# A hybrid decoder block on one core: lora products at full height with zero-padded weights, parameters read behind x, and other starting times for the planner

## The chip, the cores and the metric

The kernel runs on one core of a Trainium2 chip. The metric is the device time of one execution in microseconds (us). The engines have one queue each: TensorE (PE in the profile; PEld are its weight loads) does matrix products, VectorE (DVE), ScalarE (ACT) and GpSimd (POOL) do elementwise work, and SyncE (SP) issues the transfers (DMA) between the core's memory and HBM.

## What is computed

The reference is one decoder layer over 512 positions of width 1024: two token mixers side by side, merged by gates, and behind them a gated feed-forward layer with a short convolution. The part that the change touches is the decay and the gate `a` of the RWKV mixer; `wz` and `az` have 64 columns each, the results have 1024:

```python
z_r = z_r + rwkv_mu * (_shift1(z_r) - z_r)
rr, kr, vr, wz, az, gz = _split(z_r, [RWKV_DIM, RWKV_DIM, RWKV_DIM, W_LORA, A_LORA, G_LORA])
w_log = -jax.nn.softplus(-(rwkv_w0 + jnp.tanh(wz) @ rwkv_w2).astype(F32)) - 0.5
decay = jnp.exp(-jnp.exp(w_log))
a = jax.nn.sigmoid((rwkv_a0 + az @ rwkv_a2).astype(F32))
...
y = _rwkv7_scan(r_h, w_h, k_r, v_r, -kk, kk * a_h)
...
h = h + _rmsnorm(mix, attn_post_norm[l])
```

All of it is float32. The kernel gets that precision from products in the chip's faster float32 form (`fp32r`) by splitting each operand into a high part and a remainder: three products in place of one for the large matrices, two for the lora matrices.

## The kernel before

**Stages.** A first stage (line L399 for all of its engine instructions, since a helper records them) loads x and the parameters, splits x into `xuh` and `xul`, computes the first five column blocks of the input product into `zps`, and the norm of x. Then comes the mixer stage (line L243): 8 blocks of 128 channels (`hb`, called heads here, though each holds two RWKV heads of 64), and for each the input products of K, R, V, F, Q, G and VN (24 products with 512 columns into `zps`, or products with 256 columns into `vps`), an RWKV front, a triangular solve, an RWKV chain over 8 chunks (products into `us` and `yp`), and the HGRN mixer (`hsc`, `ups`, `ops`). 16 gate blocks and three blocks of the branch product close the stage. Behind it come the branch products, the output product and the feed-forward layer, which are not planned anew.

**What sets the order.** In the first stage the order is that of the code. In the mixer stage a planner (class `Plan`) interleaves eight generators at build time: it keeps an assumed time at which each engine is free (`at`), an assumed cost for each operation and an assumed delay between engines, and emits whichever operation can start first by its own reckoning. What it emits is then fixed: on each engine the instructions run in that order, and each waits for its inputs. `AT0` holds the assumed times at which VectorE, ScalarE and GpSimd come free, counted from the moment at which TensorE does (zero).

**The lora products.** `zwah` holds the 64 rows of tanh(wz) above the 64 rows of az, high parts; `zws` and `zas` hold remainders in one half and a second copy of the high part in the other. For each head, `front(hb)` loads the two 64-row weight matrices twice, one copy under the other (`lwr`), ScalarE makes the high part (`lw`), and GpSimd overwrites one half of it with the remainder. A product of 64 rows (`lw[0:64]` by `zwah[0:64]`) and one of 128 rows (`lw` by `zws`) are summed in `wps`; the same for `aps` with the other half.

**The first loads.** SyncE issues the transfers of the first stage in one queue: two weight blocks in halves, 8 columns of parameters, x in 8 tiles (`xt`), and the other 290 columns of parameters (`pr`) ahead of x's tiles 3 to 7. On VectorE `consts()`, twelve small operations that read those 290 columns, stands ahead of the remainders `xul` of tiles 3 to 7.

Of the kernel before, what the change touches and what calls it, by code (L numbers as in the profile page):

```python
# [8 lines left out]
F32 = mybir.dt.float32  # L9
F32R = mybir.dt.float32r  # L10
# [6 lines left out]
P = 128  # L17
# [21 lines left out]
NPRM = _off  # L39
# [5 lines left out]
RAWS = 1  # L45
WAIT, PEN = 1.0, 0.07
MARGIN = 0.8
AT0 = (5.5, 2.5, 0.0)
XG = ((0, 0),)
MORD = ((0, 0), (1, 0), (2, 0), (3, 0), (0, 1), (1, 1), (2, 1), (3, 1))  # L50
WOT = (7.0, 9.2, 13.5, 15.0)
# [235 lines left out]
def block_kernel(ctx: ExitStack, tc: tile.TileContext, out: bass.AP, xT: bass.AP, xN: bass.AP,  # L287
# [3 lines left out]
    nc = tc.nc  # L291
# [8 lines left out]
    pr = const.tile([P, NPRM], F32, name="pr")  # L300
# [5 lines left out]
    def pcs(name):  # L306
        o, w = PCOLS[name]
        return pr[:, o : o + w]
# [74 lines left out]
    pers = ph1.enter_context(tc.tile_pool(name="pers", bufs=1))  # L383
# [17 lines left out]
    Vi, Gi, Ai, Ti = Chain(V, "Vi"), Chain(G, "Gi"), Chain(A, "Ai"), Chain(T, "T")  # L401
# [39 lines left out]
    Gi.memset(r17[:, :, :, 0:1], 1.0)  # L441
    scm = pers.tile([P, NT, P], F32, name="scm")
    lwr0 = pers.tile([P, 2 * P], F32, name="lwr0")
    Gi.memset(sgx[:, :, 0:1], 0.0)
    Gi.memset(scm, 0.0)

# [13 lines left out]
    def consts():  # L460
        Vi.tensor_scalar(cm, pr[:, o_mu : o_mu + 26], -1.0, 1.0, op0=ALU.mult, op1=ALU.add)
        Vi.tensor_single_scalar(hw0, pcs("w0"), 0.5, op=ALU.mult)
        Vi.tensor_single_scalar(ha0, pcs("a0"), 0.5, op=ALU.mult)
        Vi.tensor_single_scalar(hka, pcs("k_a"), 0.5, op=ALU.mult)
        Vi.tensor_scalar(oka, pcs("k_a"), -0.5, 1.0, op0=ALU.mult, op1=ALU.add)
        Vi.tensor_single_scalar(nkk, pcs("k_k"), -1.0, op=ALU.mult)
        Vi.tensor_single_scalar(hkk, pcs("k_k"), 0.5, op=ALU.mult)
        Vi.tensor_single_scalar(lnw8, pcs("ln_w"), 8.0, op=ALU.mult)
        Vi.tensor_single_scalar(gn5, pcs("gnorm"), 0.5, op=ALU.mult)
        Vi.tensor_tensor(lmx, pcs("lb0"), pcs("lb1"), op=ALU.max)  # L470
        Vi.tensor_tensor(le[:, 0], pcs("lb0"), lmx, op=ALU.subtract)
        Vi.tensor_tensor(le[:, 1], pcs("lb1"), lmx, op=ALU.subtract)
# [38 lines left out]
    with tc.tile_pool(name="init", bufs=1) as ip, tc.tile_pool(name="pinit", bufs=1, space=PSUM) as pi:  # L511
# [26 lines left out]
        def init_wh(b, dst, src=None):  # L538
            raw = wraw.tile([P, 1024], F32, name="raw", tag="raw")
            nc.sync.dma_start(raw, win[b] if src is None else src)  # L540
            hi, lo = dst
            w0.append(dst)
            wlast["hi"] = Ai.copy(hi, raw)
            wlast[V] = Vi.tensor_tensor(lo, raw, hi.bitcast(F32), op=ALU.subtract)
# [6 lines left out]
        def half_load(i, c):  # L551
            hc = slice(c * 512, c * 512 + 512)
            nc.sync.dma_start(raws0[i][:, hc], win[(B_WA, B_GZ)[i]][:, hc])

        def half_split(i, c, eng, key):
            hc = slice(c * 512, c * 512 + 512)
            hi, lo = w0[i]
            wlast["hi"] = Ai.copy(hi[:, hc], raws0[i][:, hc])
            wlast[eng] = key.tensor_tensor(lo[:, hc], raws0[i][:, hc], hi[:, hc].bitcast(F32), op=ALU.subtract)

        def init_x(k):
            Ai.activation(xuh[:, k], xt[:, k], AF.Identity, scale=pc("g_pre", k))
            Vi.scalar_tensor_tensor(xul[:, k], xt[:, k], pc("g_pre", k), xuh[:, k].bitcast(F32),
                                    op0=ALU.mult, op1=ALU.subtract)

        def init_s(k):
            x2 = acc[k] if k < 2 else ip.tile([P, S], F32, name="x2", tag="xr", bufs=6)
            Ai.activation(x2, xt[:, k], AF.Square)
            if k > 1:
                Vi.tensor_tensor(acc[k % 2], acc[k % 2], x2, op=ALU.add)  # L570
            if k == KD - 1:
                Vi.tensor_tensor(acc[0], acc[0], acc[1], op=ALU.add)
# [15 lines left out]
            nc.sync.dma_start(xt[:, k], xT[:, k])  # L588
        half_load(0, 1)
        half_load(1, 1)  # L590
        nc.sync.dma_start(pr[:, 8:NPRM], prm[:, 8:NPRM])
        for k in range(3, KD):
            nc.sync.dma_start(xt[:, k], xT[:, k])
        half_split(0, 0, V, Vi)
        init_x(0)
        half_split(1, 0, V, Vi)
# [1 line left out]
            init_x(k)  # L598
        half_split(0, 1, V, Vi)
        half_split(1, 1, V, Vi)  # L600
        consts()
        for k in range(3, KD):
            init_x(k)
            if k >= LAG:
                init_s(k - LAG)
        init_wh(B_K, wi[0])
        for k in range(KD - LAG, KD):
            init_s(k)
# [65 lines left out]
    V1, G1, A1, T1, D1 = Lazy(V, "V"), Lazy(G, "G"), Lazy(A, "A"), Lazy(T, "T"), Lazy(nc.sync, "D")  # L674
    for k_ in "VGA":
        last[k_] = last[k_ + "i"]
    plan = Plan(seq, RANKS, BONUS, (0.0,) + AT0 + (0.0,))

# [29 lines left out]
    zwah = pers.tile([P, S], F32R, name="zwah")  # L708
# [4 lines left out]
    hs = (slice(0, 64), slice(64, 128))  # L713
# [35 lines left out]
    def front(hb):  # L749
        lwr = lwr0  # L750
        if hb > 0:
            yield D1.dma_start(lwr, wlg[hb, :, 0 : 2 * P])
        lw = mx.tile([P, 2 * P], F32R, name="lw")
        yield A1.copy(lw, lwr)
        for h in range(2):
            q, c = hs[1 - h], slice(h * P, h * P + P)
            yield G1.tensor_tensor(lw[q, c], lwr[q, c], lw[q, c].bitcast(F32), op=ALU.subtract)
        yield done(("K", hb), "zwa")
        fin.add(("go", hb))
        k = kt[hb]  # L760
        wps = pf.tile([P, S], F32, name="wps", tag="f")
        yield T1.matmul(wps, lw[0:64, 0:P], zwah[0:64], start=True, stop=False)
        yield T1.matmul(wps, lw[:, 0:P], zws, start=False, stop=True)
        sg = sgx
        yield A1.activation(sg[:, :, 1:65], c8(wps), AF.Tanh, scale=0.5, bias=hw0[:, hb : hb + 1])
        yield V1.tensor_single_scalar(sg[:, :, 1:65], sg[:, :, 1:65], 1.0, op=ALU.add)
        aps = pf.tile([P, S], F32, name="aps", tag="f")
        yield T1.matmul(aps, lw[64:128, P : 2 * P], zwah[64:128], start=True, stop=False)
        yield T1.matmul(aps, lw[:, P : 2 * P], zas, start=False, stop=True)
        cum = mx.tile([P, NCH, 65], F32, name="cum")  # L770
        yield V1.tensor_tensor_scan(cum.rearrange("p n c -> p (n c)"), m65.rearrange("p n c -> p (n c)"),
# [501 lines left out]
    plan.spawn("evac", lora_in())  # L1273
    plan.spawn("evac", first_in())
    plan.spawn("front", chained(front, lambda hb: []))
    plan.spawn("chain", chained(chain, lambda hb: [("solve", hb), "zgz"]))
    plan.spawn("hgrn", chained(hgrn, lambda hb: [("F", hb)]))
# [339 lines left out]
```

## Time and profile before

| | before |
|---|---|
| median of 3 runs | 1190.23 us (1187.6 to 1190.32) |
| the profiled execution, its own time | 1188.11 us |
| its span, from the first to the last instruction | 1186.4 us |
| PE busy | 1154.1 us (97% of the span) |
| DVE, ACT, POOL busy | 60%, 44%, 46% |
| DMA, mean over the span | 100 GB/s |

Times below are counted from the span's start. Matmuls are pipelined, so the busy time of one is longer than its slot; the slot is the distance from one start to the next. "Idle" is the time in which an engine had nothing to run, with what ended it behind the arrow; that name is taken from the semaphore that changed last and is sometimes that of another instruction that ended at the same moment. PEclk is the granted share of TensorE's full clock of 2.4 GHz, so that 0.50 is its lower level, 1.2 GHz.

### The profile page before, as it was taken

To read this page: it belongs to the slowest core of one execution; us is meant where nothing else is said; L and a number is where in the kernel's file an instruction comes from. 1 tells how busy PE (TensorE), PEld (TensorE's weight loads), DVE (VectorE), ACT (ScalarE), POOL (GpSimd) and SP (SyncE) were. 2 spreads that over 40 slices of the span, in tenths; PEclk is the share of its full clock that TensorE was granted. 3 is DMA by queue.
4 is the path that set the end of the run, shared out by engine and by line. 5 is a ranking of instruction groups with operands and counts; after the bars stand their busy time and mean duration, and the time that the engine had idled before them with its cause. 6 is when DMAs were issued, how large, how long until landed. Compare 5 with 4: busy or idle time off the path is not lost. (4 is left out here: it accounts for less than half of the span.)

```text
span 1186.4 us, 19408 instructions
## 1 busy us (share of the span) xinstructions
PE 1154.1 (97%) x7336; PEld 951.2 (80%) x7336; DVE 717.4 (60%) x1599; ACT 522.4 (44%) x1010; POOL 540.5 (46%) x572
## 2 busy tenths in 40 slices
PE   9998999999999999999999999999999999999997
PEld 7776797877878787788888778888888888888786
DVE  6898888889878778987747535445422322232213
ACT  7634355454545454454544532245433343434221
POOL 2254345353344434334343655402856575657521
PEclk9999999999999999999999999999999999999999
DMA  5212222122222131323242584373322232323232
GB/s 187 72 54 68 80 63 79 50 66 89 70 72 61 54 108 43 98 70 94 67 136 64 186 276 161 112 243 125 107 89 89 89 107 82 123 81 111 88 104 89
DMA packets 57390, 118.85 MB, mean 100 GB/s; under 512 B 22097, under 2 KB 25297, under 8 KB 57297
## 3 DMA queue, kind: packets, MB, share of 16 engines
q1 hardware_dynamic: 57296, 117.62, 31.7%
q8 instruction: 58, 0.95, 0.3%
q14 instruction: 36, 0.29, 0.1%
HBM read 104.22 MB, written 13.37 MB: 99 GB/s over the span
## 5 line engine op out<-in xcount | busy, mean ns | idle before, releaser
L243 POOL TENSOR_TENSOR wlo_t<-raw,whi_t 128x256 fp32r<-128x256 f32 x280 | 226.2, 836 | 294.8 <-ACT whi_t L243 264.6
L324 POOL TENSOR_TENSOR wlo_t<-raw,whi_t 128x1024 fp32r<-128x1024 f32 x75 | 182.2, 2436 | 84.0 <-ACT whi_t L324 83.8
L243 PE MATMUL zps<-xl,whi_t 128*128 128x512 f32 x488 | 198.4, 406 | 0.0
L243 PE MATMUL zps<-xh,wlo_t 128*128 128x512 f32 x488 | 198.1, 406 | 0.0
L243 PE MATMUL zps<-xh,whi_t 128*128 128x512 f32 x488 | 198.0, 406 | 0.0
L324 ACT CAST whi_t<-raw 128x1024 fp32r<-128x1024 f32 x77 | 80.1, 1048 | 153.4 <-DMA raw<-wup 66.6
L1478 DVE SCALAR_TENSOR_TENSOR u<-zps,pr,u 128x511 f32<-128x511 f32 x40 | 30.0, 750 | 188.1 <-ACT u L1477 184.6
L366 PE MATMUL zps<-x2h,whi_t 128*128 128x512 f32 x320 | 124.7, 390 | 0.0
L368 PE MATMUL zps<-x2h,wlo_t 128*128 128x512 f32 x320 | 124.7, 390 | 0.0
L367 PE MATMUL zps<-x2l,whi_t 128*128 128x512 f32 x320 | 124.5, 389 | 0.0
L243 ACT CAST whi_t<-raw 128x1024 fp32r<-128x1024 f32 x74 | 77.4, 1046 | 79.1 <-PE zps L243 23.9
L243 PEld LDWEIGHTS zps<-xh,whi_t 128*128 128x128 f32 x488 | 92.1, 189 | 17.8 <-issue 1.0
L243 PEld LDWEIGHTS zps<-xh,wlo_t 128*128 128x128 f32 x488 | 92.2, 189 | 17.5 <-issue 0.7
L243 PEld LDWEIGHTS zps<-xl,whi_t 128*128 128x128 f32 x488 | 92.3, 189 | 16.5 <-issue 0.7
L367 PEld LDWEIGHTS zps<-x2l,whi_t 128*128 128x128 f32 x320 | 60.1, 188 | 12.7
L368 PEld LDWEIGHTS zps<-x2h,wlo_t 128*128 128x128 f32 x320 | 60.1, 188 | 12.6
L366 PEld LDWEIGHTS zps<-x2h,whi_t 128*128 128x128 f32 x320 | 60.1, 188 | 12.6
L1503 POOL TENSOR_TENSOR th<-th,u 128x512 f32<-128x512 f32 x22 | 28.4, 1292 | 71.8 <-DVE u L1479 71.8
L1477 ACT ACTIVATE u<-zps,pr 128x512 f32<-128x512 f32 x40 | 30.9, 775 | 39.0 <-PE zps L368 39.0
L243 PEld LDWEIGHTS yp<-sv,X 128*128 128x128 f32 x256 | 37.0, 190 | 7.0 <-DVE sv L243 3.2
L367 PE MATMUL yps<-ol,whi_t 128*128 128x512 f32 x104 | 41.0, 394 | 1.7 <-DVE ol L324 1.7
L243 ACT COPY ys<-us 64x128 f32<-64x128 f32 x64 | 16.7, 260 | 58.1 <-DVE sv L243 50.5
(393 smaller groups left out, 2650.6 us busy)
## 6 DMA issues: line engine op xcount, KB each, us to landing
raw<-win SPq DMA_DIRECT2D x64, 512.0 KB, 3.7
raw<-wup SPq DMA_DIRECT2D x44, 512.0 KB, 3.6
raw<-wdn SPq DMA_DIRECT2D x22, 512.0 KB, 3.5
raw<-wbr SPq DMA_DIRECT2D x16, 512.0 KB, 4.2
raw<-whi SPq DMA_DIRECT2D x8, 512.0 KB, 3.7
sg_d<-sg SPq DMA_DIRECT2D x16, 256.0 KB, 2.4
gate<-sg_d SPq DMA_DIRECT2D x8, 512.0 KB, 5.7
raw<-wout SPq DMA_DIRECT2D x8, 512.0 KB, 3.5
```

The source lines that it names most:

```text
L243: op.ins_ = self.seq(op.key, op.fn(*op.args, **op.kw))
L324: return A.copy(hi, raw), eng.tensor_tensor(lo, raw, hi.bitcast(F32), op=ALU.subtract)
L366: T.matmul(o, lh, rh, start=start, stop=False)
L367: T.matmul(o, lh, rl, start=False, stop=False)
L368: T.matmul(o, ll, rh, start=False, stop=stop)
L1477: A.activation(u, ps, AF.Identity, scale=pc("cw2", b), bias=pc("cb", b))
L1478: V.scalar_tensor_tensor(u[:, 1:S], ps[:, 0 : S - 1], pc("cw1", b), u[:, 1:S], op0=ALU.mult, op1=ALU.add)
L1503: G.tensor_tensor(th, th, uv_, op=ALU.mult)
```

## The change

Three edits. The high part of the lora weights gets a tile of its own, `lwh`, 128 rows high, zeroed once by GpSimd; for each head ScalarE casts 64 rows for `wps` and 64 rows for `aps` into it, and the products that had 64 rows now have 128, by the whole of `zwah`, of which the other half meets zeros. In the first stage the 290 columns of parameters are read behind x, and `consts()` moves behind the remainders of all x tiles. And the planner starts from `AT0 = (7.0, 5.0, 2.0)`.

```diff
-AT0 = (5.5, 2.5, 0.0)
+AT0 = (7.0, 5.0, 2.0)
...
+    lwh = pers.tile([P, 2 * P], F32R, name="lwh")
+    Gi.memset(lwh.bitcast(F32), 0.0)
...
-        nc.sync.dma_start(pr[:, 8:NPRM], prm[:, 8:NPRM])
         for k in range(3, KD):
             nc.sync.dma_start(xt[:, k], xT[:, k])
+        nc.sync.dma_start(pr[:, 8:NPRM], prm[:, 8:NPRM])
...
         half_split(1, 1, V, Vi)
-        consts()
         for k in range(3, KD):
             init_x(k)
             if k >= LAG:
                 init_s(k - LAG)
+        consts()
         init_wh(B_K, wi[0])
...
         for h in range(2):
+            yield A1.copy(lwh[hs[h], h * P : h * P + P], lwr[hs[h], h * P : h * P + P])
+        for h in range(2):
             q, c = hs[1 - h], slice(h * P, h * P + P)
             yield G1.tensor_tensor(lw[q, c], lwr[q, c], lw[q, c].bitcast(F32), op=ALU.subtract)
...
-        yield T1.matmul(wps, lw[0:64, 0:P], zwah[0:64], start=True, stop=False)
+        yield T1.matmul(wps, lwh[:, 0:P], zwah, start=True, stop=False)
         yield T1.matmul(wps, lw[:, 0:P], zws, start=False, stop=True)
...
-        yield T1.matmul(aps, lw[64:128, P : 2 * P], zwah[64:128], start=True, stop=False)
+        yield T1.matmul(aps, lwh[:, P : 2 * P], zwah, start=True, stop=False)
         yield T1.matmul(aps, lw[:, P : 2 * P], zas, start=False, stop=True)
```

The planner's order changes over the whole mixer stage. Three places are shown; in each, rows are instructions in the order in which the engine runs them, out<-in.

VectorE in the first stage. Before, `consts()` (from `cm` to `le`) stands behind the remainders of the two weight blocks, and the four remainders `xul` of tiles 3 to 6 come next:

```order
L399 TENSOR_TENSOR wlo_t<-raw,whi_t 128x512 x2
L399 TENSOR_SCALAR cm<-pr 128x26
L399 TENSOR_SCALAR hw_130<-pr 128x8
L399 TENSOR_SCALAR ha_131<-pr 128x8
L399 TENSOR_SCALAR hka<-pr 128x8
L399 TENSOR_SCALAR oka<-pr 128x8
L399 TENSOR_SCALAR nkk<-pr 128x8
L399 TENSOR_SCALAR hkk<-pr 128x8
L399 TENSOR_SCALAR lnw_136<-pr 128x8
L399 TENSOR_SCALAR gn_137<-pr 128x8
L399 TENSOR_TENSOR lmx<-pr 128x8
L399 TENSOR_TENSOR le<-pr,lmx 128x8 x2
```

Now, at the same place:

```order
L399 TENSOR_TENSOR wlo_t<-raw,whi_t 128x512 x2
L399 SCALAR_TENSOR_TENSOR xul<-xt,pr,xuh 128x512 x4
L399 TENSOR_TENSOR acc_165<-acc_165,x_224 128x512
L399 SCALAR_TENSOR_TENSOR xul<-xt,pr,xuh 128x512
L399 TENSOR_TENSOR acc_166<-acc_166,x_229 128x512
L399 TENSOR_SCALAR cm<-pr 128x26
```

The remainders follow at once; the twelve operations stand behind the last of them.

TensorE at the first lora product of head 0, in the VN block (`vps`) at the start of the mixer stage. Before, 79 products into `vps` stand ahead of the first row with `wps`:

```order
L243 MATMUL vps<-whi_t,xh 128x256
L243 MATMUL wps<-zwah,lw 128x512
L243 MATMUL vps<-wlo_t,xh 128x256
L243 MATMUL vps<-whi_t,xl 128x256
L243 MATMUL wps<-zws,lw 128x512
L243 MATMUL vps<-whi_t,xh 128x256
```

Now 90 stand ahead of it:

```order
L243 MATMUL wps<-zwah,lwh 128x512
L243 MATMUL vps<-whi_t,xh 128x256
L243 MATMUL vps<-wlo_t,xh 128x256
L243 MATMUL vps<-whi_t,xl 128x256
L243 MATMUL vps<-whi_t,xh 128x256
L243 MATMUL vps<-wlo_t,xh 128x256
L243 MATMUL vps<-whi_t,xl 128x256
L243 MATMUL wps<-zws,lw 128x512
```

The first of the pair has moved behind 11 more products, and between the two stand 6 instead of 2.

ScalarE ahead of head 1's lora products (`lw` is their weight, `X` and `v` are evacuations that stand beside it, `sgx` reads the result). Before:

```order
L243 CAST whi_t<-raw 128x1024
L243 COPY X_746<-tp 128x4x2x64
L243 CAST lw<-lwr_126 128x256
L243 ACTIVATE v<-zps,cm 128x512
L243 CAST whi_t<-raw 128x1024
L243 ACTIVATE sgx<-wps,hw_130 128x8x64
```

Now:

```order
L243 CAST whi_t<-raw 128x1024
L243 ACTIVATE v<-zps,cm 128x512
L243 COPY X_759<-tp 128x4x2x64
L243 CAST lw<-lwr_126 128x256
L243 CAST lwh<-lwr_126 64x128 x2
L243 ACTIVATE sgx<-wps,hw_132 128x8x64
L243 CAST whi_t<-raw 128x1024
```

The evacuation `v` and the two new casts now stand ahead of the point at which the product can start; the next weight block's cast has moved behind `sgx`. On TensorE two `zps` products that stood between `ups` and `wps` are gone, nine stand between `wps` and `aps`, and `ops` comes behind `aps` instead of ahead of it.

## Rows read from the trace of the kernel before

**Rows 1.** The page's first part: busy time, share of the span and number of instructions of each engine.

```profile
PE 1154.1 (97%) x7336; PEld 951.2 (80%) x7336; DVE 717.4 (60%) x1599; ACT 522.4 (44%) x1010; POOL 540.5 (46%) x572
```

**Rows 2.** Busy time by stretches of the span: from:to, length, then busy us (instructions) of PE, PEld, DVE, ACT and POOL, the granted share of TensorE's clock, the DMA share and GB/s.

```profile
11.20:14.10 2.90, 1.40 (x5) 0.78 (x5) 2.87 (x16) 2.68 (x5) 0.00 (x0) 1.00 1.02 333
14.20:17.40 3.20, 3.20 (x9) 2.43 (x8) 2.82 (x5) 3.20 (x6) 0.00 (x0) 0.50 0.55 210
...
40.00:51.70 11.70, 10.22 (x82) 9.72 (x80) 10.37 (x15) 7.25 (x12) 5.13 (x6) 1.00 0.17 47
...
99.00:106.20 7.20, 3.60 (x19) 2.47 (x18) 7.17 (x11) 3.00 (x5) 6.19 (x9) 1.00 0.27 76
106.40:109.60 3.20, 3.20 (x9) 2.15 (x8) 2.93 (x11) 2.18 (x10) 1.26 (x3) 0.50 0.00 0
109.80:500.00 390.20, 378.37 (x3152) 309.36 (x3150) 332.18 (x881) 195.44 (x448) 165.92 (x233) 1.00 0.24 71
500.00:656.00 156.00, 156.00 (x1250) 132.14 (x1250) 109.38 (x314) 75.18 (x180) 64.83 (x93) 1.00 0.27 82
656.00:691.00 35.00, 33.92 (x156) 27.82 (x155) 15.11 (x17) 16.24 (x29) 21.22 (x24) 1.00 0.71 236
```

**Rows 3.** The waits of TensorE, longest in total first: what waited, for what, us in total, times, longest.

```profile
PE vp L243 <- DVE ys L243: 3.6, 3, 1.3
PE yt L243 <- DVE ys L243: 3.5, 3, 1.5
PE ops L243 <- DVE st L243: 2.1, 1, 2.1
...
PE wps L243 <- POOL wlo_t L243: 1.6, 1, 1.6
...
PE wps L243 <- POOL lw L243: 1.0, 1, 1.0
```

**Rows 4.** The first stage, in order of time, on three engines (start, us, engine, line, operation; idle before it in brackets), and the transfer of the 290 columns.

```profile
11.03 0.40 PE L399 MATMUL zps<-xuh,wlo_t 128*128 128x512 f32 x1
12.20 0.50 PE L399 MATMUL zps<-xuh,whi_t 128*128 128x512 f32 x1 [0.77 <-ACT xuh L399]
13.42 0.50 PE L399 MATMUL zps<-xul,whi_t 128*128 128x512 f32 x1 [0.72 <-DVE xul L399]
...
11.42 1.40 ACT L399 ACTIVATE xuh<-xt,pr 128x512 fp32r<-128x512 f32 x2 [0.47 <-DMA xt<-xT]
...
12.62 2.13 DVE L399 SCALAR_TENSOR_TENSOR xul<-xt,pr,xuh 128x512 fp32r<-128x512 f32 x3
...
pr<-prm SPq DMA_DIRECT2D x1, 145.0 KB, 6.2
```

**Rows 5.** TensorE's starts at two places where chunk products (`us`, four records) are followed by products in the faster form: by two of 128 rows, and by a lora pair whose first has 64 rows (64*128).

```profile
211.52 0.39 PE L243 MATMUL zps<-xh,whi_t 128*128 128x512 f32 x1
211.74 0.55 PE L243 MATMUL us<-sv,X 128*128 128x64 f32 x4
212.10 0.48 PE L243 MATMUL zps<-xl,whi_t 128*128 128x512 f32 x1
212.42 0.39 PE L243 MATMUL zps<-xh,wlo_t 128*128 128x512 f32 x1
...
299.59 0.56 PE L243 MATMUL us<-sv,X 128*128 128x64 f32 x4
300.08 0.49 PE L243 MATMUL aps<-zwah,lw 64*128 64x512 f32 x1
300.50 0.50 PE L243 MATMUL aps<-zas,lw 128*128 128x512 f32 x1
300.85 0.39 PE L243 MATMUL zps<-xl,whi_t 128*128 128x512 f32 x1
```

**Rows 6.** Head 0's first lora products: TensorE, and what they read on ScalarE.

```profile
51.82 0.46 PE L243 MATMUL wps<-zwah,lw 64*128 64x512 f32 x1 [1.55 <-POOL wlo_t L243]
...
53.09 0.47 PE L243 MATMUL wps<-zws,lw 128*128 128x512 f32 x1 [0.37 <-ACT zws L243]
...
51.12 0.60 ACT L243 CAST zwah<-zwa 128x512 fp32r<-128x512 f32 x1
...
52.37 0.62 ACT L243 CAST zws<-zwa 64x512 fp32r<-64x512 f32 x1
```

**Rows 7.** Head 1's lora products and the HGRN products behind them, on four engines.

```profile
98.90 0.58 ACT L243 COPY X<-tp 128x512 f32<-128x512 f32 x1
99.38 0.41 ACT L243 CAST lw<-lwr 128x256 fp32r<-128x256 f32 x1
99.68 0.69 ACT L243 ACTIVATE v<-zps,cm 128x512 f32<-128x512 f32 x1
...
101.61 3.88 DVE L243 TENSOR_TENSOR nb<-nb,tmp 64x54 f32<-64x54 f32 x1
...
100.86 1.14 POOL L243 TENSOR_TENSOR lw<-lwr,lw 64x128 fp32r<-64x128 f32 x2
101.97 3.45 POOL L243 TENSOR_TENSOR wlo_t<-raw,whi_t 128x256 fp32r<-128x256 f32 x5
...
106.04 0.60 PE L243 MATMUL ops<-st,qi 128*128 128x128 f32 x2 [2.13 <-DVE st L243]
```

**Rows 8.** ScalarE's group of instructions nearest to the new casts (the same cast with as many columns): line, engine, operation, shapes, count, busy us, mean ns, idle before them.

```profile
L243 ACT CAST lgh<-lgr 128x128 fp32r<-128x128 f32 x8 | 2.3, 292 | 0.2
```

## The prediction

> **What bounds the kernel now.** I read the busy times first, then the stretches, the waits of TensorE, and the timelines where the waits lie. TensorE is busy 97% of the span [rows 1], so the question for every edit is whether it takes slots or waits from TensorE. In the last quarter of the mixer stage, 500 to 656 us, TensorE has no idle time, and from 656 to 691 it idles 1.1 us of 35 [rows 2]: the gate blocks fill what the mixers leave, and a slot saved earlier arrives at the end of the stage. From 109.8 to 500 us it idles 11.8 us of 390, with VectorE busy for 85% [rows 2]; there the mixers' own chain is close behind TensorE. The waits are short and scattered [rows 3], except at three places that the edits touch: the first stage, head 0's first lora product, and the stretch from 99 to 106.2 us, in which TensorE is busy for 3.6 us of 7.2 [rows 2]. Twice the granted clock is 0.50 (1.2 GHz), from about 14.2 to 17.4 and from 106.4 to 109.6 us, each time just behind waits [rows 2].
>
> **The lora products at full height.** Sixteen products change from 64 to 128 rows. From the four chunk products through a 64-row product and its partner, a pair takes 300.85 − 299.59 = 1.26 us. With full products in both places it takes 0.36 us for the chunk products, 0.32 for the first product behind them and 0.22 for the second, 0.90 in all [rows 5]. So a change is worth 0.36: 0.20 in its own slot (0.42 against 0.22) and the rest at its edges, where the array goes from one height to another. Sixteen times 0.36 is 5.8 us. The bounds are 3.2 (own slots alone, if the edges stay) and 7.4 (both edges of 0.13, 0.49 against 0.36 and 0.35 against 0.22 in those rows, and no dearer slot behind chunk products).
>
> Here a rule speaks against the change. The Trainium skill, page "TensorE: Matmul & The Clock Gate", section "Why this matters for your kernels", says that a single matmul with few rows takes as long as one with all 128. By it only the edges would be saved, 16 × 0.16 = 2.6 us. The trace disagrees: the 64-row slot is 0.42 us, the full one 0.22 [rows 5]. The edges agree with the page "TensorEngine Tiling (Array Packing)", section "Tiling Modes", by which a change of tiling mode drains the engine.
>
> The price is two casts of 64×128 for each head on ScalarE. The nearest row, the same cast with as many columns, takes 0.29 us [rows 8]: 16 × 0.29 = 4.7 us on an engine that is busy 44% [rows 1]. They cost nothing where ScalarE waits anyway; where a lora product waits for them, each pair delays it by up to 0.6 us. The zeroing of `lwh` is one GpSimd instruction in the first stage, where GpSimd is idle from 11.2 to 17.4 us [rows 2]; nothing.
>
> **The parameters behind x.** Tile 3 of x ends ScalarE's wait of 0.47 at 11.42 [rows 4]. The 145 KB ahead of it take, at the 333 GB/s of that stretch [rows 2], about 0.4 us (an estimate from those two rows), so `xuh` of tile 3 starts at about 11.0 and TensorE's product with it at 11.8 in place of 12.20. Its remainder `xul` then needs only `xuh`, two of which take 1.40 [rows 4]: it can start at 11.75, not 12.62, and TensorE's second product comes at about 12.55 in place of 13.42. TensorE's waits of 0.77 and 0.72 shrink to some 0.35 and 0.25: 0.87 us saved. `consts()` goes behind the last remainder, where VectorE has some 1 us less cover ahead of the sum of squares; the norm needs that later, and TensorE has K's products in between. I take nothing for it; without that cover it is the 1.0 us of the twelve operations.
>
> Then the clock. It fell right behind these two waits, and the 3.2 us at 0.50 [rows 2] cost half, 1.6 us. With 0.6 us of waits in place of 1.5, I expect it not to fall; the bound is nothing.
>
> **The starting times.** With later assumed times the planner puts the first product of head 0 behind 11 more `vps` products. One takes 10.22/82 = 0.12 us [rows 2], so it comes 1.3 us later in TensorE's queue. It waited 1.55, in truth for `zwah`, which ended at 51.72 [rows 6]: some 0.2 is left. Its partner waits for `zws`, which ends at 52.99 [rows 6]; with six products between, TensorE would reach it at about 52.75, so 0.3 is left of 0.37. Saved: 1.4 us.
>
> At head 1 the second wait for `lw` is 1.0 us [rows 3], after 0.4 for the first. The new order has `v` ahead of `X`, `lw` and the two casts. From the start of the `tp` products ScalarE then needs about 2.2 us (0.69, 0.58, 0.41 and two casts, overlapping a little [rows 7, 8]) against TensorE's 1.0, so some 1.2 us of wait comes ahead of the first product and, with GpSimd's 1.14 for the remainder [rows 7], 0.4 ahead of the second: 1.6 in place of 1.4, 0.2 lost. What is behind it gains. VectorE's small `nb` operation took 3.88 us, beginning with GpSimd's run of splits and ending as the fifth split ended (101.97 + 3.45 = 105.42 against 105.49), and `ops` waited 2.13 for the scan behind it [rows 7]. In the new order `ops` stands behind nine `zps` products and the `aps` pair, some 2.5 us, and the next block's split begins only behind `sgx`; I take the 2.1 as saved, and the 1.6 of the clock that followed [rows 2]. Bounds: nothing, if VectorE is locked out there again, and 3.7.
>
> The other waits [rows 3] are of the mixers' chain; the order around `yt` and `vp` has about as many products between as before, so I leave them. The bounds are 4 us to either side.
>
> **Sum.** 5.8 + 0.9 + 1.6 + 1.4 + 2.1 + 1.6 − 0.2 = 13.2 us. On the profiled execution's own time that is 1188.1 − 13.2 = 1174.9; it lies 2.1 us under the median of the runs shown, so against the median I put 1177.
>
> **Rivals.**
>
> *The chain sets the pace.* Between 109.8 and 500 us VectorE is 85% busy. If the chain and not TensorE is the limit there, the slots saved at heads 2 to 7 turn into waits: 12 × 0.36 = 4.3 us less, 1181. The same time comes out if neither clock period goes away (3.2 less, 1180). For it: the chain's waits in [rows 3]. Against it: 500 to 656 us without idle time.
>
> *The height is no matter* (the rule above): 3.2 us less, 1180. The slots in [rows 5] speak against it.
>
> *The new order brings new waits of the old size.* The 11.8 us of idle time from 109.8 to 500 double: 1189, no change that can be told. The order is new everywhere behind head 0, and its assumed costs know nothing of a lockout such as the one at 101.61.
>
> *Slower.* The longer ScalarE queue ahead of `wps` is met at every head, as at head 1: 1.6 us of wait, and 1.6 us of clock behind it as at 106.4, 3.2 for each. At heads 2 to 7 that is 19 us, and 1196; it decides from five of these heads on. Against it: before, `wps` waits at heads 0 and 1 alone.
>
> **Numbers.** Less than 0.3% (3.6 us) can hardly be told from no change by these runs. The forecast has 0.50, the chain or the clock 0.27, the height 0.03, new waits 0.13, slower 0.07. Faster is the first three, 0.80; same 0.13; slower 0.07. The range goes from 1171 (lora at its upper bound, the scattered waits down by 4) to 1188, just short of the case of new waits; the likeliest case alone is 1172 to 1182.
>
> **What would show it.** Lora products with slots of 0.22 to 0.32 us and no 64*128 form. In the first stage `xul` of tile 3 at about 11.8 and no 0.50 near 14 us. Head 0's `wps` pair with about 0.5 us of wait. From 99 to 110 us no `nb` of several us and a clock of 1.00. Idle time from 110 to 500 us near 12 us. The prediction is wrong if that idle time grows by what the lora products give, or if waits ahead of `wps` appear at later heads.

## The result, and the profile after

The changed kernel takes 1182.41 us (median of 4 runs, 1180.86 to 1183.13) against 1190.28 for the kernel before in the same session: a ratio of 0.9937, with a 95% interval from 0.9920 to 0.9955. That is 7.9 us less; 13.2 were forecast. A second measurement of the same program (below) gave 0.9948 (0.9928 to 0.9968); where "the changed kernel" is compared, it stands for the mean of both, 0.994, about 6.9 us.

The profiled execution took 1183.13 us, with a span of 1181.0. TensorE is as busy a share of the span as in [rows 1]:

```profile
PE 1150.6 (97%) x7336; PEld 950.7 (80%) x7336; DVE 721.6 (61%) x1599; ACT 527.1 (45%) x1026; POOL 544.4 (46%) x573
```

Busy time by stretches, columns as in [rows 2]; the stretches begin and end at the same events as there or at the same times:

```profile
11.20:14.10 2.90, 2.81 (x12) 1.98 (x11) 2.27 (x4) 2.90 (x6) 0.00 (x0) 1.00 1.02 325
38.10:100.10 62.00, 58.00 (x384) 47.87 (x382) 53.10 (x107) 29.52 (x48) 26.67 (x30) 0.94 0.22 65
100.10:667.60 567.50, 554.18 (x4501) 459.15 (x4502) 461.82 (x1223) 286.42 (x670) 253.37 (x347) 0.99 0.27 79
...
77.80:84.60 6.80, 6.62 (x25) 5.43 (x26) 6.74 (x14) 0.00 (x0) 3.23 (x4) 0.50 0.00 0
125.60:128.90 3.30, 3.30 (x9) 2.56 (x8) 3.26 (x7) 0.00 (x0) 0.00 (x0) 0.50 0.00 0
299.70:303.00 3.30, 3.30 (x17) 3.20 (x17) 3.22 (x7) 2.15 (x4) 1.99 (x3) 0.50 0.11 17
109.80:500.00 390.20, 381.57 (x3228) 317.13 (x3226) 340.21 (x897) 199.55 (x468) 171.32 (x236) 0.99 0.25 73
656.00:687.10 31.10, 27.65 (x121) 22.02 (x121) 11.87 (x14) 13.59 (x21) 18.96 (x20) 1.00 0.71 229
```

The kernel before, for the two stretches that [rows 2] does not have: from its first `vps` product to head 1's first lora product, and from there to the first product of the branch block (`zps<-oh`).

```profile
40.30:99.80 59.50, 56.58 (x384) 45.83 (x382) 51.89 (x108) 28.59 (x45) 25.26 (x29) 1.00 0.23 67
99.80:674.70 574.90, 558.78 (x4505) 460.85 (x4506) 462.75 (x1227) 285.85 (x664) 248.69 (x348) 1.00 0.27 80
```

The branch block, from its first product to the end of the mixer stage, before and in the changed kernel:

```profile
674.70:691.10 16.40, 16.40 (x74) 13.55 (x74) 3.41 (x4) 5.66 (x7) 10.29 (x12) 1.00 0.69 233
...
667.60:687.10 19.50, 17.73 (x78) 14.10 (x77) 4.88 (x6) 8.34 (x13) 10.97 (x12) 1.00 0.66 225
```

Four things are to be seen in this pair of executions. The first stage is 2.2 us shorter (first `vps` product at 38.1, before at 40.3), but head 1's first lora product comes at 100.1, before at 99.8: head 0 takes longer by as much. From there to the branch block it takes 567.5 us in place of 574.9, 7.4 less. Of this 3.1 are given back in the branch block, which has four products more in it and waits for its input `oh` (1.4 us, below); with the 0.3 lost ahead of head 1, the mixer stage ends 4.0 us earlier (687.1 against 691.1). The other 1.4 us between the two spans lie in the stages behind, which no edit touches; over the traces of all the kernels here these take 492.6 to 495.4 us. And the clock, which fell at 14 and 106 us before, now fell at 78, 126 and 300 us: 13.4 us at 0.50 in these three rows, 6.4 in the two of [rows 2]. Every trace has one more fall, in its last few us.

The waits of TensorE, as in [rows 3]:

```profile
PE yt L243 <- DVE ys L243: 3.9, 5, 1.7
PE wps L243 <- ACT lwh L243: 2.3, 2, 1.4
PE scb L243 <- DVE bk L243: 2.2, 1, 2.2
PE dps L243 <- DVE Tn L243: 1.8, 1, 1.8
PE vp L243 <- DVE ys L243: 1.6, 1, 1.6
PE zps L243 <- ACT oh L243: 1.4, 1, 1.4
...
PE ops L243 <- DVE st L243: 1.1, 2, 0.7
...
PE wps L243 <- POOL wlo_t L243: 0.3, 1, 0.3
```

The lora waits that the prediction named are there in about the sizes that it gave (head 0: 0.3; `ops`: 1.1 in place of 2.1), but `scb` (0.1 us at that place before) and `dps` (0.4) are new at this size. The place of the `scb` wait, on VectorE and TensorE, before:

```profile
77.62 0.69 DVE L243 TENSOR_TENSOR bk<-k,cum 64x512 f32<-64x512 f32 x1
...
78.36 0.37 PE L243 MATMUL scb<-X,bk 64*128 64x128 f32 x1
```

and now, on GpSimd, VectorE and TensorE:

```profile
75.28 5.75 POOL L243 TENSOR_TENSOR wlo_t<-raw,whi_t 128x256 fp32r<-128x256 f32 x6
...
75.96 0.84 DVE L243 TENSOR_TENSOR qi<-hq,p 128x256 f32<-128x256 f32 x1
76.81 1.12 DVE L243 TENSOR_TENSOR bk<-k,cum 64x512 f32<-64x512 f32 x1
...
77.98 0.58 PE L243 MATMUL scb<-X,bk 64*128 64x128 f32 x1 [2.23 <-DVE bk L243]
```

VectorE ends `bk` at 77.93 us, before at 78.31. TensorE reaches the product at 75.75 (77.98 − 2.23) in place of 78.28, with eight products more ahead of it: what it won up to here it spends waiting for VectorE. In the new order six of GpSimd's splits stand back to back just where VectorE makes the last operands of head 0's `scb` products; the `bk` row took 1.12 us there, before 0.69, and on the other half, outside of that stretch, 0.62.

### The profile page after: what moved, and what is told of

Same layout as the page of the kernel before. It is cut to its first block, busy times and chain, and to the rows that moved or that the text cites. A ratio compares the mean times of both kernels' runs of the same rounds, so it can differ in the third digit from the quotient of the medians.

```text
span 1181.0 us, 19441 instructions
## 1 busy us (share of the span) xinstructions
PE 1150.6 (97%) x7336; PEld 950.7 (80%) x7336; DVE 721.6 (61%) x1599; ACT 527.1 (45%) x1026; POOL 544.4 (46%) x573
## 5 line engine op out<-in xcount | busy, mean ns | idle before, releaser
L243 POOL TENSOR_TENSOR wlo_t<-raw,whi_t 128x256 fp32r<-128x256 f32 x280 | 229.7, 848 | 300.3 <-ACT whi_t L243 281.1
L243 PE MATMUL zps<-xh,whi_t 128*128 128x512 f32 x488 | 200.5, 411 | 0.0
L243 PEld LDWEIGHTS us<-sv,X 128*128 128x128 f32 x256 | 37.3, 190 | 6.0 <-DVE sv L243 1.7
```

The source lines that it names most:

```text
L243: op.ins_ = self.seq(op.key, op.fn(*op.args, **op.kw))
```

## The experiments

Ratios are to the kernel before on the same chip and in the same session; its medians were 1188.4 to 1188.9 us. The clock is the mean granted share over the executions of a kernel; the kernel before had 0.995 in each of these sessions.

| kernel | median us | ratio, 95% interval | clock |
|---|---|---|---|
| changed kernel, again | 1182.9 | 0.9948 (0.9928 to 0.9968) | 0.9946 |
| half height in the changed order | 1184.8 | 0.9975 (0.9963 to 0.9987) | 0.9949 |
| lora edit alone | 1193.7 | 1.0062 (1.0038 to 1.0085) | 0.9893 |
| starting times alone | 1186.2 | 0.9986 (0.9973 to 0.9998) | 0.9961 |
| first-stage edit alone | 1189.4 | 1.0012 (0.9998 to 1.0025) | 0.9946 |
| first-stage edit undone | 1182.3 | 0.9934 (0.9916 to 0.9952) | 0.9948 |
| fillers at two waits | 1184.8 | 0.9967 (0.9955 to 0.9979) | 0.9959 |
| fillers at seven waits | 1185.3 | 0.9967 (0.9951 to 0.9984) | 0.9973 |
| 15 products more at head 0 | 1183.7 | 0.9957 (0.9939 to 0.9976) | 0.9955 |
| 15 products more at head 5 | 1185.4 | 0.9969 (0.9953 to 0.9985) | 0.9931 |
| starting times (6.5, 4.5, 1.5) | 1186.9 | 0.9988 (0.9978 to 0.9999) | 0.9933 |
| lora weights early | 1188.6 | 0.9995 (0.9979 to 1.0011) | 0.9905 |

**Half height in the changed order.** The two costs in the planner are set so that it reckons with full height; every engine then has exactly the order of the changed kernel.

```diff
-                    op.us *= 1.86
+                    op.us *= 1.0
...
-        yield T1.matmul(wps, lwh[:, 0:P], zwah, start=True, stop=False)
+        yield T1.matmul(wps, lwh[0:64, 0:P], zwah[0:64], start=True, stop=False)
...
-        yield T1.matmul(aps, lwh[:, P : 2 * P], zwah, start=True, stop=False)
+        yield T1.matmul(aps, lwh[64:128, P : 2 * P], zwah[64:128], start=True, stop=False)
```

> The changed kernel with one thing undone: the sixteen high-part products have 64 rows again (half of lwh by half of zwah), and the planner's costs are set so that every engine runs its instructions in exactly the order of the changed kernel. Theory (each product of 64 rows costs TensorE 0.36 us more, and this is on the path): 5.8 us slower than the changed kernel, about 1188, and the slots at the lora products as in the kernel before. Rival 1 (the mixers' chain sets the pace, and saved slots turn into waits): under 3 us slower, 1185 or less. Rival 2 (a product with few rows takes as long, only the edges cost): 2.6 us slower, 1185.

Measured: 0.9975 against 0.994, 3.9 us slower, uncertain by about 2. That excludes that the height is worth nothing, and by itself none of the three theories. The same place of the two programs, head 5's `aps` pair on TensorE, with half height:

```profile
372.54 0.40 PE L243 MATMUL zps<-xh,wlo_t 128*128 128x512 f32 x1
372.86 0.50 PE L243 MATMUL aps<-zwah,lwh 64*128 64x512 f32 x1
373.29 0.51 PE L243 MATMUL aps<-zas,lw 128*128 128x512 f32 x1
373.63 0.39 PE L243 MATMUL zps<-xh,whi_t 128*128 128x512 f32 x1
```

and in the changed kernel:

```profile
373.25 0.39 PE L243 MATMUL zps<-xh,wlo_t 128*128 128x512 f32 x1
373.49 0.39 PE L243 MATMUL aps<-zwah,lwh 128*128 128x512 f32 x1
373.72 0.40 PE L243 MATMUL aps<-zas,lw 128*128 128x512 f32 x1
373.95 0.40 PE L243 MATMUL zps<-xh,whi_t 128*128 128x512 f32 x1
```

Three slots take 1.09 us (373.63 − 372.54) in place of 0.70 (373.95 − 373.25): 0.39 for one product where rival 2 had 0.16: 0.20 in its own slot (0.43 against 0.23) and 0.19 in the slots beside it. At ten of the sixteen places the difference is 0.32 to 0.50, at the other six, beside waits or chunk products, 0.13 to 0.24. Over all of them, waits taken out, it adds up to 5.1 us. The time shows 3.9, and its uncertainty takes in the 5.1. The stretch from head 2's first lora product to the first of the branch block, with half height and in the changed kernel:

```profile
160.50:667.70 507.20, 497.61 (x4003) 410.29 (x4003) 404.67 (x1095) 256.77 (x604) 221.47 (x305) 1.00 0.27 80
...
162.60:667.60 505.00, 494.74 (x4003) 410.83 (x4002) 405.58 (x1095) 257.03 (x605) 221.29 (x305) 1.00 0.27 80
```

The twelve products in it make 2.2 us, each trace with one clock stretch of 3.4 us, where the slots of these twelve add up to 4.2. So the price per product is about as predicted, and in this pair of traces half of it arrives. TensorE's idle time in the stretch is 9.6 us (507.20 − 497.61) against 10.3, so that shorter waits explain 0.7 of the 2.0 that are missing; the rest stays open.

**Each part alone.** The lora edit alone (with the old starting times and loads):

> The kernel before with the lora edit alone: old starting times, old place of the parameters. Theory (the height is worth about 6 us whatever the order): 5 to 7 us faster than before, 1183 to 1185. Rival (the new starting times are what gained, and the lora slots are lost in waits): within 2 us of before, 1188 or more.

Measured: 1.0062, 7.4 us slower than before. It isn't the height that costs: the planner's costs know of it, so that this edit gives another order too, and in this one the chain of head 7 ends late. TensorE has no gate blocks left to put in its wait:

```profile
677.68 0.66 PE L243 MATMUL yt<-ident,ys 128*128 128x128 f32 x2 [8.41 <-DVE ys L243]
```

Before, the wait at this place was 1.1 us, one of the three that stand in [rows 3] with 3.5. Both theories fell. It is also the kernel with the lowest mean clock (0.9893). An order can cost more than the sixteen products give.

The starting times alone:

> The kernel before with the new starting times alone. Theory (the new order takes waits away at heads 0 and 1 and makes others of the same sum, with clock periods of their own): within 2.5 us of before, 1188 to 1193. Rival (the step of the prediction, 1.4 + 2.1 + 1.6 us saved at heads 0 and 1): 5 us faster, 1185.

Measured: 0.9986, 1.7 us faster (0.2 to 3.2): the theory's size, not the 5 us of the prediction's step. Its trace has `scb` waiting 1.7 and `ops` 1.8 us, so that the new `scb` wait comes with the starting times.

The first-stage edit alone, with the mixers in the order of before:

> The kernel before with the first-stage edit alone (parameters read behind x, consts() behind the remainders); the order of the mixer stage is that of before. Theory (0.9 us of waits and 1.6 us of the clock saved in the first stage, nothing given back later): 2.2 to 2.5 us faster than before, 1188. Rival (the mixer stage's own chain takes it back as waits): within 1 us of before, with the first stage shorter by 2 us all the same.

Measured: 1.0012, no gain (0.2 us faster to 3.0 slower); the rival's. In its trace the first stage ends at 38.3, head 1's first lora product comes at 99.3, and the clock was at 0.50 for 3.4 us at 52 us, behind the wait ahead of head 0's `wps`. The same edit, undone in the changed kernel:

```diff
+        nc.sync.dma_start(pr[:, 8:NPRM], prm[:, 8:NPRM])
         for k in range(3, KD):
             nc.sync.dma_start(xt[:, k], xT[:, k])
-        nc.sync.dma_start(pr[:, 8:NPRM], prm[:, 8:NPRM])
...
         half_split(1, 1, V, Vi)
+        consts()
...
-        consts()
```

> The changed kernel with the first-stage edit undone (parameters ahead of x's tiles 3 to 7, consts() ahead of their remainders); the order of the mixer stage is that of the changed kernel. Theory (the first stage gets 2 us longer again, but the mixers' chain at heads 0 and 1 does not wait for TensorE, so that little of it arrives): within 1.5 us of the changed kernel, which stood at 0.9937 and 0.9948 of before. Rival (the step of the prediction, 0.9 us of waits and 1.6 of the clock): 2 to 2.5 us slower, 0.996 to 0.997 of before.

Measured: 0.9934, the time of the changed kernel. The step of the prediction, 2.5 us, is refuted twice. Its trace has the first `vps` product at 39.2 and no clock stretch in the first stage. Over all traces that product comes at 37.6, 38.1, 39.2 and 40.3 us in the four kernels without the edit and at 38.0 to 39.2 in the ten traces with it: one execution differs from the next by as much as the edit was to save, and the trace that the prediction read is the latest of all.

**The changed kernel again.**

> The changed kernel once more, unaltered, beside the three others of this call and with more executions. Theory (16 products at 0.36 us, of which the half-height kernel showed 3.6 us): 0.993 to 0.995 of before, and a mean granted clock of 0.994. Rival (the first measurement was a lucky draw): 0.996 or more, no faster than the half-height kernel.

Measured: 0.9948, clock 0.9946. Of the first trace's three clock stretches ahead of the feed-forward layer only the one at 78 us is there (3.4 us long in place of 6.8); behind the `dps` wait, 1.84 us in both, the clock stayed at 1.00, and there is one at 676 us that the first did not have. What is the program's are the waits; whether the clock falls behind one of them differs from one execution to the next.

**Fillers.** A hook in the planner's emission puts products of a zero weight into the open block ahead of a chosen instruction; they stand in no cost and change no order:

```diff
+    FILL = {("scb", 0): 9, ("dps", 0): 7}
+    def fill(op):
+        label = op.outs[0].tensor.name.rpartition("_")[0]
+        n = seen[label] = seen.get(label, -1) + 1
+        for _ in range(FILL.get((label, n), 0)):
+            seq("T", T.matmul(opened[0], zero, xh[:, 0], start=False, stop=False, skip_group_check=True))
```

> The changed kernel with products of a zero weight, added into the column block that is open, ahead of two waits of TensorE behind which the clock fell in the trace: nine (2.0 us) ahead of the first scb product of head 0 (a wait of 2.23), seven (1.6 us) ahead of the first dps product of head 0 (1.84). They change no result and no order. Theory (the clock falls since TensorE waits there, and each fall costs half its length): no stretch of 0.50 near 78 and 126 us, 3 to 5 us faster than the changed kernel, about 1178. Rival 1 (the fall belongs to the stretch, not to the wait, or moves to the next wait): the mean clock stays at 0.994 and the time within 1.5 us. Rival 2 (the fillers delay what waits behind them): slower by up to 3.6 us.

> As the kernel with fillers, and with more of them at five further waits (five ahead of wps of head 1, three ahead of its ops, four ahead of yt of head 0, four ahead of wps of head 4, five ahead of the last column of the branch block). Theory: no stretch of 0.50 before the feed-forward layer, clock 0.997, 5 us faster than the changed kernel, about 1177. Rival (waits of about 1 us did not bring the clock down, so that these fillers only get in the way): no faster than with the first two, or up to 2 us slower.

Measured: both 0.9967, 2 to 3 us slower than the changed kernel, each uncertain by about 2.5. The mean clock did rise, from 0.9946 to 0.9959 and 0.9973, and the more so the more waits were filled, as it should where the clock falls since TensorE waits; with two waits filled the stretches at 78 and 126 are gone, and others are there at 100, 298 and 677; with seven, one at 299 is left ahead of the feed-forward layer. But no time came with it. 0.0027 of 1183 us (seven waits filled) are 3.2 us of the clock's price given back, and the kernel was slower by 2.4 than the changed kernel of the same session. Part of the reason is shown by the stretch from head 0's first lora product to that of head 1 (the table below): it takes 50 us with and without a fall, so that what a fall costs there is taken from a wait. The stretch from head 2 to the branch block, too, took 505.0 us in the changed kernel's first trace, with 3.4 us at the lower clock, and 505.1 in its second, with none. That is no rule for the whole program: over the 206 executions of these sessions, within each kernel, 0.001 less of the mean clock goes with 0.85 us more (an estimate, by a line through the listed times and clocks, uncertain by about 0.12), where 1.19 would be the price if every us at 0.50 cost half. Why the filled kernels are not faster, or are slower, isn't settled: from head 2 to the branch block, where it has the changed kernel's instructions and no filler, the one with two waits filled takes 506.5 us in its trace against 505.1 in the changed kernel's second, and its clock stretch of 6.8 us at 298 explains that in this execution, but over the executions its clock is the higher one.

**Where slots count.** Five traces with the changed order had taken 50.0 to 50.8 us from head 0's first lora product to head 1's, and so I put fifteen zero products (3.5 us) into head 0's column blocks, or into head 5's.

```diff
+    FILL = {("zps", 24 + 24 * b + 4 * i): 1 for b in range(3) for i in range(1, 6)}
```

> The changed kernel with fifteen more products of a zero weight (15 x 0.23 = 3.5 us of TensorE) spread over the three column blocks of head 0, from about 59 to 75 us. Theory (there the mixers' chain on VectorE sets the pace and TensorE waits for it, so slots cost little; the five kernels with the changed order all took 50.0 to 50.8 us from the first lora product of head 0 to that of head 1, with 0, 3.4 or 6.8 us at the lower clock): at most 1.5 us slower than the changed kernel. Rival (TensorE sets the pace there too): 3.5 us slower.

> The same fifteen products (3.5 us of TensorE) spread over three column blocks of head 5, from about 386 to 401 us, where TensorE of the changed kernel waited 0.27 us in 71. Theory (TensorE sets the pace there): 3 to 3.5 us slower than the changed kernel, about 0.997 of before. Rival (the chain sets the pace there too, with waits hidden in the slots of its own products): under 1.5 us slower.

Measured: 1.7 us slower at head 0 (0.9957), 3.2 at head 5 (0.9969), each uncertain by about 2.5, so that the times alone don't tell the two apart; the traces do. Head 0 with fifteen products more, from its first lora product to that of head 1:

```profile
49.20:99.00 49.80, 47.18 (x310) 37.49 (x308) 41.37 (x93) 21.94 (x35) 21.78 (x25) 1.00 0.23 69
```

Head 5 with fifteen more, and below it head 5 of the changed kernel:

```profile
369.10:443.60 74.50, 74.35 (x584) 60.89 (x582) 59.40 (x166) 37.89 (x90) 32.91 (x44) 1.00 0.27 78
```

```profile
370.30:441.80 71.50, 71.23 (x569) 57.86 (x567) 59.19 (x166) 37.91 (x90) 32.87 (x44) 1.00 0.28 81
```

Head 0 takes 49.8 us with them and 49.7 to 50.5 without; the wait ahead of `scb` is filled by them and gone. Head 5 takes 3.0 us more. The traces read so at head 0 (first lora product of head 0, that of head 1, time at the lower clock between them):

| trace | head 0 | head 1 | length | at 0.50 |
|---|---|---|---|---|
| before | 51.8 | 99.8 | 48.0 | 0 |
| first-stage edit alone | 49.8 | 99.3 | 49.5 | 3.4 |
| changed kernel | 49.6 | 100.1 | 50.5 | 6.8 |
| changed kernel, again | 50.3 | 100.5 | 50.2 | 3.4 |
| first-stage edit undone | 50.3 | 100.4 | 50.1 | 3.4 |
| half height | 49.7 | 100.1 | 50.4 | 0 |
| 15 products more at head 0 | 49.2 | 99.0 | 49.8 | 0 |
| 15 products more at head 5 | 49.5 | 99.2 | 49.7 | 0 |
| fillers at two waits | 49.7 | 99.7 | 50.0 | 0 |
| fillers at seven waits | 49.9 | 100.8 | 50.8 | 0 |

The first two rows have the order of before. In the eight others, which have the changed order, head 0 takes 49.7 to 50.8 us, with 0 to 15 products more in it and with 0, 3.4 or 6.8 us at the lower clock: TensorE's work doesn't set its length. A head 0 that begins 1 us earlier does end earlier, by 1.4 us (49.2 and 99.0 against 50.3 and 100.4), so that time saved ahead of it isn't lost by that. What VectorE waited for TensorE between 49 and 87 us, before and in the changed kernel:

```profile
DVE rn L243 <- PE nps L243: 2.2, 1, 2.2
...
DVE rn L243 <- PE nps L243: 0.2, 1, 0.2
```

It is 0.2 to 0.6 us in the eight traces, and 3.5 in that of the first-stage edit alone, with its fall at 52 us. So in the order of before TensorE did hold VectorE up in head 0. In the new one it hardly does: in the changed kernel's first trace VectorE is busy for 33.1 of these 38 us, and its longer waits are for ScalarE (4.5 us in all). Why head 0 is 2 us longer in the new order than the 48.0 of before isn't separated.

**What TensorE waits for at head 1.** The wait's name is `lwh`, so the last kernel casts the next head's lora weights early:

```diff
-    def front(hb):
-        lwr = lwr0
+    def lora_w(hb):
+        lwr = lwr0
...
+    def front(hb):
+        yield done(("lw", hb))
+        lw = lws[hb]
...
+        if hb < HB - 1:
+            plan.spawn("front", lora_w(hb + 1))
```

> The changed kernel with the next head's lora weights read and cast as soon as this head's aps products are done, in place of at the start of the next head. It takes away what wps waited for at heads 1 and 4 (1.4 and 0.9 us in the first trace, 2.7 and 0.9 in the second), and gives the planner another order. Theory (waits for lwh end, the other waits of the chain stay as they are in sum): no wait ahead of wps behind head 0, 1 to 3 us faster than the changed kernel, about 1180. Rival 1 (the chain behind is late anyway and the wait goes to the next product that reads its results): within 1.5 us. Rival 2 (the new order is a draw): anywhere from 1178 to 1190, with other waits as the reason.

Measured: 0.9995; rival 2, and the theory's own step fell as well. The wait is still there. ScalarE and TensorE of this kernel:

```profile
98.18 1.04 ACT L243 CAST whi_t<-raw 128x1024 fp32r<-128x1024 f32 x1 [2.15 <-DMA raw<-win]
...
99.62 0.58 ACT L243 COPY X<-tp 128x512 f32<-128x512 f32 x1
...
100.25 0.59 PE L243 MATMUL wps<-zwah,lwh 128*128 128x512 f32 x1 [2.61 <-ACT X L243]
```

`wps` and `tp` share one bank of PSUM (the pool `pf`, tag `f`, one buffer), and `tp` is copied out by ScalarE (`X<-tp`) behind a cast of weights that have not landed. In the kernel with seven waits filled a zero product into `wps`, which reads no lora weight, waits there as well:

```profile
99.52 1.43 PE L1292 MATMUL wps<-xh,zero 128*128 128x512 f32 x5 [1.68 <-ACT X L246]
```

The changed kernel's second trace shows the same, with SyncE's queue ahead of it:

```profile
87.14 4.81 SPq L243 DMA_DIRECT2D lb_d<-X  x8
93.17 0.52 SPq L243 DMA_DIRECT2D nb<-lb_d  x1
93.78 0.52 SPq L243 DMA_DIRECT2D raw<-win  x1
...
97.88 1.04 ACT L243 CAST whi_t<-raw 128x1024 fp32r<-128x1024 f32 x1 [1.15 <-DMA raw<-win]
...
99.42 0.57 ACT L243 COPY X<-tp 128x512 f32<-128x512 f32 x1
...
100.54 0.49 PE L243 MATMUL wps<-zwah,lwh 128*128 128x512 f32 x1 [2.67 <-ACT lwh L243]
```

and the kernel before, too:

```profile
87.29 4.88 SPq L243 DMA_DIRECT2D lb_d<-X  x8
...
94.01 0.52 SPq L243 DMA_DIRECT2D raw<-win  x1
...
97.95 1.05 ACT L243 CAST whi_t<-raw 128x1024 fp32r<-128x1024 f32 x1 [1.99 <-DMA raw<-win]
```

So what sets 100 us is a row of things on several engines: VectorE finishes the first part of head 0's `X` at 87; eight small stores of it take SyncE's queue for 4.8 us; the read of them waits behind; only then is the next weight block read, whose cast starts 4.1 us after that issue; and ScalarE's queue holds `tp` behind it. In all fourteen traces the first of these stores begins at 85.7 to 87.6 us and head 1's first lora product follows 12.1 to 13.7 us later. This is read from the traces and was not tested by moving that load. What made this kernel as slow as the one before isn't shown either; its longest single wait is new, 4.4 us of `vp` at 276 us, and its mean clock is 0.9905.

The starting times in between:

> The changed kernel with the planner's starting times at (6.5, 4.5, 1.5) in place of (7.0, 5.0, 2.0): half a us, far less than the length of any wait here, but the order of the whole mixer stage is another. Theory (an order is a draw; its sum of waits and clock stretches has nothing to do with the size of the step): a time more than 3 us away from the changed kernel's is as likely as not, anywhere from 1179 to 1192. Rival (the times set how well the planner's reckoning fits, and half a us is a small error): within 1.5 us of the changed kernel.

Measured: 0.9988, 5.4 us slower than the changed kernel, for half a us in an assumed time. `yt` alone waits 9.1 us in six times there (3.9 in the changed kernel). An order is a draw, as the theory has it; how wide the draw is, three orders at these costs (0.994, 0.9988, and 1.0062 with the old times) show.

```profile
PE yt L243 <- DVE ys L243: 9.1, 6, 3.9
PE scb L243 <- DVE bk L243: 3.1, 2, 1.7
```

## Why the prediction was right or wrong

The sign and the range were right. The sum was 13.2 us and the gain 6.9 to 7.9; by its terms:

| term | forecast | what the runs show |
|---|---|---|
| lora height | 5.8 (3.2 to 7.4) | 5.1 at the slots, 3.9 (± 2) in time |
| first-stage waits | 0.9 | no gain in time, in either order |
| clock in the first stage | 1.6 | 0; without the edit no fall there in another execution, and the mean clock is no higher |
| head 0's lora waits | 1.4 | 1.6 at the place, 2.2 lost again ahead of `scb` |
| head 1's `wps` | −0.2 | 1.40 in all against 1.46: +0.1 (−1.2 in the second trace) |
| head 1's `ops` | 2.1 | 1.0 (0.71 + 0.40 left) |
| clock behind it | 1.6 | 0 |
| the rest of the order | 0 | not separated; the order as a whole 1.7 (alone) to 3.0 (half height against before) |

The four terms of the starting times (1.4, −0.2, 2.1 and 1.6) make 4.9 us, and the whole order gave 1.7 to 3.0. The traces don't show that this came from the places that the prediction named. The time lies in the range because the range was wide and the lora term held; of the other terms none is shown, so that the range was met in part by luck.

**Right: the lora products.** A product of full height has a slot of 0.23 us, as read from [rows 5] (0.22), and the sixteen together were worth 5.1 us at their places, 3.9 (± 2) in time. The price of 2.6 us, edges alone, is refuted at the places; the time by itself doesn't exclude it. By the Trainium skill (page "TensorE: Matmul & The Clock Gate", section "Why this matters for your kernels") a single matmul with few rows takes as long as a full one. The 64-row slot is longer here, 0.43 against 0.23 us in the same order; but a change of height stands at its end each time, and no run has two such products in a row, so that the product's own time and the change are not told apart, and the prediction's "the trace disagrees" says too much.

**Wrong: "a slot saved earlier arrives at the end".** The prediction said it on the strength of 500 to 656 us, where TensorE had no idle time, and used it for the first stage and head 0. There it fails. In the changed order TensorE reached head 0's `scb` products 2.5 us earlier and waited 2.2 for VectorE's `bk`, and head 0 takes as long with fifteen products more. At head 1 it then waits for a row of stores, a load and a copy that begins with VectorE's `X`. The sign of it was in [rows 2], where TensorE was busy for half of the 7.2 us from 99 on, and [rows 7] has the copy of `tp` that began at 98.90; I read these waits as belonging to the lora weights' queue on ScalarE and did not ask what that queue waited for. The rival of the chain was weighed for heads 2 to 7 alone. There it was partly right: 2.2 of 4.2 us arrived in one pair of traces. At the end of the stage the step fails again: in the branch block 3.1 us of the 7.4 were given back.

**Wrong: the first stage as a saving.** Of the 0.9 us of waits no run shows a gain in time. The waits themselves became shorter in the trace, 0.4 and 0.3 us in place of 0.77 and 0.72, but the stage's length differs by up to 2.7 us between the traces without the edit (37.6 to 40.3), and the forecast was made from the longest.

**Wrong: the clock.** The prediction took two falls away and put none in their place. In the traces a fall stands behind waits, the new order has its own of these (`scb` 2.23, `dps` 1.84), and the mean clock was 0.995 before and 0.994 to 0.995 after. So the 3.2 us of the forecast were no gain.

**Wrong: the other waits unchanged.** The rival of new waits was right in kind, with `scb`, `dps` and `oh`, and VectorE is slowed beside GpSimd's splits at `bk` at 76.8 us in place of `nb` at 101.6. It wasn't right in place or size: from 109.8 to 500 us TensorE idles 8.6 us (390.20 − 381.57), before 11.8; from 500 to 656 us 1.9, before nothing; and from 656 to 687 us 3.5, before 1.1.

**The slower case** did not come: `wps` waits at heads 1 and 4 (1.4 and 0.9 us), not at five heads. The prediction named a wait ahead of `wps` at a later head as a sign of being wrong; the one at head 4 is such a wait.

## What to carry to other kernels

Before a saving is booked, look for the next place where the engine waits, and ask what that wait's last cause is, through the queues behind the name in the row: where another engine's chain sets the time of that place, slots saved ahead of it turn into waiting. Where a planner sets the order, an edit of its costs or starting times is a draw of several us, so that the edit and the order have to be measured apart, here by keeping the order and undoing the edit. A clock fall that shows in one trace is no property of the program, nor is the length of a stage that differs by 2 us between executions: average the granted clock over executions, and read a stage in several traces, before a term is made of either.

## What was not expected of the hardware

The same wait (`dps`, 1.84 us) is followed by a fall of the clock to 1.2 GHz in one execution and by none in another of the same program. Filling waits raised the mean clock (0.9946, 0.9959, 0.9973) and did not shorten the time. Eight stores from 16 partitions each hold SyncE's queue for 4.8 us; in the changed kernel's second trace seven of them took 0.3 to 0.4 us each and one 1.6. The cast of a 0.5 MB weight block whose read stands behind them starts 4.1 us after that issue (93.78 to 97.88). VectorE was slowed through six GpSimd instructions in a row (5.75 us): `bk` 1.12 in place of 0.62 us, and three `kj` operations of 64 columns 0.74 to 0.77, where the next one, behind the last split, took 0.21.
